# The weight slots of a float32r decoder trunk are moved by 128 bytes in SBUF

## The chip, the cores and the metric

The kernel runs on one core of a Trainium2 chip. The metric is the device time of one execution in microseconds (us), the median of several runs; lower is better. TensorE (PE) multiplies, VectorE (DVE) and ScalarE (ACT) do the elementwise work, GpSimd (POOL) a few small operations, and SyncE (SP) issues the DMAs. Operands of PE lie in SBUF, which has 128 partitions; an address below is a byte offset inside a partition, the same in all partitions.

## The reference

Two layers; in each a SwiGLU half, a mixer and a second SwiGLU half act on a residual stream of 512 tokens by 1024 channels, in float32.

```python
D_MODEL = 1024; SEQ = 512; DEPTH = 2; D_FF = 2816; IN_PROJ_WIDTH = 2560

def _swiglu(h, w_gate, w_up, w_down):
    return (jax.nn.silu(h @ w_gate) * (h @ w_up)) @ w_down

def _mixer(h, w_in, conv_w, pool_w, pool_scale, w_out):
    proj = h @ w_in
    q, k, v, gate_b, gate_c, conv_h, pool_in = jnp.split(proj, SPLIT_POINTS, axis=-1)
    ...
    return jnp.concatenate([attn, conv, pool], axis=-1) @ w_out

def reference(x, norm_g, ffn_w_gate, ffn_w_up, ffn_w_down, w_in, conv_w, pool_w, pool_scale, w_out):
    for l in range(DEPTH):
        g = norm_g[l]
        f = _swiglu(_rmsnorm(x, g[0]), ffn_w_gate[l, 0], ffn_w_up[l, 0], ffn_w_down[l, 0])
        x = x + 0.5 * _rmsnorm(f, g[1])
        m = _mixer(_rmsnorm(x, g[2]), w_in[l], conv_w[l], pool_w[l], pool_scale[l], w_out[l])
        x = x + _rmsnorm(m, g[3])
        f = _swiglu(_rmsnorm(x, g[4]), ffn_w_gate[l, 1], ffn_w_up[l, 1], ffn_w_down[l, 1])
        x = x + 0.5 * _rmsnorm(f, g[5])
    return x
```

The attention is a causal stick-breaking attention of 8 heads of 64 channels; the short convolution has 3 taps, and the pooling mixer applies a 64 by 64 map to each of four groups.

## The kernel before

Every product is made of three float32r matmuls: each operand is split into a high part (rounded to float32r) and a low part (the rest), and high times high, high times low and low times high are summed in PSUM. All of them go through the helper `mm` (L224 in the profile); the order of the matmuls is fixed by hand, since each is made to follow the one before.

The weights are cut into 324 units of 128 partitions by up to 1024 columns. A unit is loaded by a DMA (`load`, L147) into a slot `raw`, ACT rounds it into a second slot `wh` (L155), and DVE subtracts to make `wl` in a third (L156). There are 28 slots of 4096 bytes per partition, in the pool `wpool`. The same slots also hold the hidden layer (`hid`, high part in the first 2048 bytes and low part in the rest), the mixer's `q`, `qk`, `v` and `mix`, the sums `f` and the gains `g`.

The normalised, transposed input of a stage lies in `hh` and `hl` (high and low part, 8 blocks of 512 tokens each, 16384 bytes each), in the pool `cpool`, which stands ahead of the slots. Behind the slots comes `apool` with the temporaries `t`, `pH`, `pL` and `c`.

In a gate, up or input projection (`unit`) the stationary operand of a matmul is a 128 by 128 piece of `wh` or `wl`, and the moving operand a block of `hh` or `hl`, 512 columns (256 in the first blocks of a stage). In a down or output projection (`token_mms`) the stationary operand is a piece of `hid` or `mix` and the moving one 512 columns of `wh` or `wl`. In the `v` projection `hh` or `hl` is stationary and `wh` or `wl` moves. In the attention `pH` and `pL` move over the constants `ntri` and `none_` of `cpool`, and over `v`. A profile's row names the moving operand first: `psz<-hh,wh` has `hh` moving and `wh` stationary. The weights of a matmul are loaded into PE (PEld) while the matmul before it runs, so the two read SBUF at the same time.

`cpool` holds, in this order and each in bytes per partition: `cst` 256, `x` 16384, `mat` 3584, `hh` 16384, `hl` 16384, `ntri`, `none_`, `identr` and `maskr` 512 each, and `expo` 256, of which one column of 4 bytes is used (the exponent of POOL's reciprocal root, L313). From the start of `hh` to the first slot are therefore 16384 + 16384 + 4 x 512 + 256 = 35072 bytes, which is 137 x 256, and from `hl` 73 x 256. Pieces of the operands lie whole multiples of 512 bytes into their tiles. So all the operands named so far begin at the same place modulo 256; only the tiles `c`, 2112 bytes apart, begin elsewhere.

## Time and profile before

| | |
|---|---|
| three runs | 1925.33, 1927.86, 1929.93 us |
| median | 1927.86 us |
| the profiled execution, its own time | 1927.51 us |
| its span from the first to the last instruction | 1925.7 us |
| PE busy | 1884.1 us (98% of the span), 9072 matmuls |
| weight loads (PEld) | 1588.2 us (82%), 9072 |
| DVE busy | 856.5 us (44%) |
| ACT busy | 714.0 us (37%) |
| DMA | 26.7% of 16 engines' span, 178.76 MB |
| PE's granted clock | 0.992 of full on average |

The profiled execution's own time is 1.8 us above its span. Matmuls are pipelined: one of 512 columns lasts some 390 ns in the records, and the next starts before it ends. What one costs in a row of them is therefore read from the distance of their starts, not from their duration.

### The profile page before, as it was taken

To read this page: it belongs to the slowest core of one execution; us is meant where nothing else is said; L and a number is where in the kernel's file an instruction comes from. 1 tells how busy PE (TensorE), PEld (TensorE's weight loads), DVE (VectorE), ACT (ScalarE), POOL (GpSimd) and SP (SyncE) were. 2 spreads that over 40 slices of the span, in tenths; PEclk is the share of its full clock that TensorE was granted. 3 is DMA by queue.
4 is the path that set the end of the run, shared out by engine and by line. 5 is a ranking of instruction groups with operands and counts; after the bars stand their busy time and mean duration, and the time that the engine had idled before them with its cause. 6 is when DMAs were issued, how large, how long until landed. Compare 5 with 4: busy or idle time off the path is not lost.

```text
span 1925.7 us, 21947 instructions
## 1 busy us (share of the span) xinstructions
PE 1884.1 (98%) x9072; PEld 1588.2 (82%) x9072; DVE 856.5 (44%) x1090; ACT 714.0 (37%) x1089; POOL 38.6 (2%) x68
## 2 busy tenths in 40 slices
PE   7999999999998999999999999999999999999998
PEld 6888888888878888888898888887888888888886
DVE  4422343567766323333463232336577563323333
ACT  3323222347764323222342322234577542222221
POOL 0000000000001000000000000000000000000000
PEclk8999999999999999999999999999999999999999
DMA  5323232131123213233142322322111232222311
GB/s 207 110 77 109 85 136 83 60 118 44 44 99 110 99 66 131 78 110 110 44 154 88 109 77 87 133 87 99 67 50 44 83 142 88 100 86 87 132 66 44
DMA packets 50645, 180.17 MB, mean 94 GB/s; under 512 B 5744, under 2 KB 5872, under 8 KB 50544
## 3 DMA queue, kind: packets, MB, share of 16 engines
q1 hardware_dynamic: 50544, 178.76, 26.7%
q8 instruction: 71, 1.16, 0.2%
q14 instruction: 30, 0.25, 0.0%
HBM read 176.65 MB, written 2.10 MB: 93 GB/s over the span
## 4 chain that ended last, share of the span: by engine, by line
PE 92%; DVE 4%; ACT 2%; DMA 1%; issue 1%; SPq 0%; POOL 0%; DVEq 0%; POOLq 0%; ACTq 0%
PE psz L224 80%; PE psd L224 10%; DMA raw<-in_w_dram 1%; DVE wl L156 1%; PE psd L266 1%; ACT t L297 1%; DVE pL L510 0%; DVE t L542 0%; ACT t L539 0%; ACT pH L509 0%; DVE hl L332 0%; DVE f L358 0%; DVE pH L507 0%; ACT wh L155 0%; DVE f L322 0%
## 5 line engine op out<-in xcount | busy, mean ns | idle before, releaser
L224 PE MATMUL psz<-hl,wh 128*128 128x512 f32 (+1 forms) x1536 | 566.9, 369 | 6.3 <-DVE hl L332 5.4
L224 PE MATMUL psz<-hh,wh 128*128 128x512 f32 (+1 forms) x1536 | 567.2, 369 | 4.1 <-ACT hh L331 4.1
L224 PE MATMUL psz<-hh,wl 128*128 128x512 f32 (+1 forms) x1536 | 566.2, 369 | 0.0
L156 DVE TENSOR_TENSOR wl<-raw,wh 128x1024 fp32r<-128x1024 f32 x324 | 386.6, 1210 | 318.1 <-ACT wh L155 248.5
L224 PE MATMUL psz<-wh,hid 128*128 128x512 f32 x1408 | 437.2, 390 | 0.0
L155 ACT CAST wh<-raw 128x1024 fp32r<-128x1024 f32 x324 | 328.7, 1039 | 233.0 <-PE psz L224 178.3
L224 PEld LDWEIGHTS psz<-hl,wh 128*128 128x128 f32 x1536 | 292.4, 190 | 54.6 <-DVE hl L332 6.1
L224 PEld LDWEIGHTS psz<-hh,wh 128*128 128x128 f32 x1536 | 292.2, 190 | 52.2 <-ACT hh L331 5.2
L224 PEld LDWEIGHTS psz<-hh,wl 128*128 128x128 f32 x1536 | 292.2, 190 | 47.5
L224 PEld LDWEIGHTS psz<-wh,hid 128*128 128x128 f32 x1408 | 264.4, 188 | 54.6
L224 PE MATMUL psz<-wl,hid 128*128 128x512 f32 x704 | 274.0, 389 | 0.0
L445 DVE TENSOR_TENSOR t<-t,psz 128x512 f32<-128x512 f32 x84 | 57.7, 687 | 470.5 <-PE psz L224 470.5
L446 ACT CAST hid<-t 128x512 fp32r<-128x512 f32 x88 | 54.6, 620 | 451.0 <-DVE t L445 451.0
L297 ACT ACTIVATE t<-psz 128x512 f32<-128x512 f32 (+1 forms) x136 | 77.5, 572 | 227.2 <-PE psz L224 226.3
L224 PEld LDWEIGHTS psz<-wl,hid 128*128 128x128 f32 x704 | 132.2, 188 | 27.3
L224 PE MATMUL psd<-hh,wh 128*128 128x512 f32 (+1 forms) x320 | 119.7, 374 | 0.0
L224 PE MATMUL psd<-hh,wl 128*128 128x512 f32 (+1 forms) x320 | 118.1, 369 | 0.0
L224 PE MATMUL psd<-hl,wh 128*128 128x512 f32 (+1 forms) x320 | 118.0, 369 | 0.0
L447 DVE TENSOR_TENSOR hid<-t,hid 128x512 fp32r<-128x512 f32 x88 | 60.9, 692 | 60.8 <-ACT hid L446 60.8
L224 PEld LDWEIGHTS psd<-hh,wl 128*128 128x128 f32 x320 | 60.3, 189 | 10.2
L224 PEld LDWEIGHTS psd<-hl,wh 128*128 128x128 f32 x320 | 60.4, 189 | 10.1 <-issue 0.5
L224 PEld LDWEIGHTS psd<-hh,wh 128*128 128x128 f32 x320 | 60.4, 189 | 10.0 <-PE psd L224 0.5
(99 smaller groups left out, 1374.2 us busy)
## 6 DMA issues: line engine op xcount, KB each, us to landing
raw<-in_w_dram SPq DMA_DIRECT2D x316, 512.0 KB, 3.3
g<-in_gains_dram SPq DMA_DIRECT2D x12, 512.0 KB, 5.1
x<-in_xt_dram SPq DMA_DIRECT2D x4, 512.0 KB, 8.4
raw<-in_w_dram SPq DMA_DIRECT2D x8, 256.0 KB, 2.8
out_dram<-x SPq DMA_DIRECT2D x8, 256.0 KB, 2.1
mat<-in_mats_dram SPq DMA_DIRECT2D x1, 384.0 KB, 9.3
mat<-in_mats_dram SPq DMA_DIRECT2D x1, 64.0 KB, 3.2
cst<-in_consts_dram SPq DMA_DIRECT2D x1, 25.0 KB, 9.1
```

Source lines behind the costliest of these rows:

```text
L155: nc.scalar.copy(h[:, :n], raw[:, :n])
L156: nc.vector.tensor_tensor(lo[:, :n], raw[:, :n], f32(h[:, :n]), op=ALU.subtract)
L224: ins = nc.tensor.matmul(dst, w, r, start=start, stop=stop, skip_group_check=True)
L266: ins = nc.tensor.transpose(dst, src, ident)
L297: ins = nc.scalar.activation(out_, in_, f_, **kw)
L445: nc.vector.tensor_tensor(u, g, pu, op=ALU.mult)
L446: nc.scalar.copy(t[:, 0, :], u)
L447: nc.vector.tensor_tensor(t[:, 1, :], u, f32(t[:, 0, :]), op=ALU.subtract)
```

## The change

The tile `expo` is declared 96 columns wide in place of 64. One column of it is used, as before, so 128 bytes more lie unused behind it. The pools behind `cpool` begin 128 bytes later: from `hh` to the first slot are now 35200 bytes, which is 137 x 256 + 128. In the built programs the first slot stands at 71808 before and at 71936 now (128 and 0 modulo 256), while `hh`, `hl` and the constants stay where they were (128 modulo 256). Slots keep their distance from each other and from `t`, `pH`, `pL` and `c`. On every engine the instructions are the same and stand in the same order.

```diff
@@ -194,7 +194,7 @@
     none_ = cpool.tile([P, P], F32R, name="none_")
     identr = cpool.tile([P, P], F32R, name="identr")
     maskr = cpool.tile([P, P], F32R, name="maskr")
-    expo = cpool.tile([P, 64], F32, name="expo")[:, 0:1]
+    expo = cpool.tile([P, 96], F32, name="expo")[:, 0:1]
     nc.vector.memset(expo, -0.5)
```

## Rows read from the trace of the kernel before

**Rows 1.** The page: busy time by engine, granted clock in 40 slices, chain that ended last.

```profile
PE 1884.1 (98%) x9072; PEld 1588.2 (82%) x9072; DVE 856.5 (44%) x1090; ACT 714.0 (37%) x1089; POOL 38.6 (2%) x68
...
PEclk8999999999999999999999999999999999999999
...
PE 92%; DVE 4%; ACT 2%; DMA 1%; issue 1%; SPq 0%; POOL 0%; DVEq 0%; POOLq 0%; ACTq 0%
```

**Rows 2.** The chain in order of time: start us, us, what.

```profile
3.05 8.78 DMA raw<-in_w_dram
...
594.55 5.42 DMA raw<-in_w_dram
...
625.34 14.40 PE psz L224 x120
...
642.62 316.23 PE psz L224 x1395
...
1333.94 5.99 DMA raw<-in_w_dram
...
1543.09 5.24 DMA raw<-in_w_dram
```

**Rows 3.** Timeline of PE, three stretches: start us, us, engine, line, operation, tiles.

```profile
58.80 0.40 PE L224 MATMUL psz<-hh,wh 128*128 128x512 f32 x1
...
113.23 0.39 PE L224 MATMUL psz<-wh,hid 128*128 128x512 f32 x1
...
156.75 0.39 PE L224 MATMUL psz<-hh,wh 128*128 128x512 f32 x1
```

**Rows 4.** Groups of PE, 4.4 to 7.9 us: count | busy us, mean ns | idle before.

```profile
L224 PE MATMUL psd<-t 128*128 128x512 bf16 x17 | 3.8, 379 | 0.0
```

**Rows 5.** Timeline of PE, 4.4 to 7.8 us, the same matmuls.

```profile
4.07 3.83 PE L224 MATMUL psd<-t 128*128 128x512 bf16 x17
```

**Rows 6.** The page: costliest groups of matmuls and weight loads.

```profile
L224 PE MATMUL psz<-hl,wh 128*128 128x512 f32 (+1 forms) x1536 | 566.9, 369 | 6.3 <-DVE hl L332 5.4
...
L224 PEld LDWEIGHTS psz<-hl,wh 128*128 128x128 f32 x1536 | 292.4, 190 | 54.6 <-DVE hl L332 6.1
...
L224 PE MATMUL psd<-hl,wh 128*128 128x512 f32 (+1 forms) x320 | 118.0, 369 | 0.0
```

**Rows 7.** Groups by form of PE and PEld, the smaller ones.

```profile
L224 PE MATMUL psz<-wh,hh 128*128 128x512 f32 x64 | 25.3, 395 | 0.0
...
L224 PEld LDWEIGHTS psz<-pH,none__73 128*128 128x128 f32 x96 | 18.5, 192 | 0.6
...
L224 PEld LDWEIGHTS psz<-pH,ntri 128*128 128x128 f32 x48 | 9.1, 190 | 1.8 <-DVE pH L507 1.2
```

**Rows 8.** Timeline of PE around three of the four products of `c` and `mat`.

```profile
489.69 1.02 PE L224 MATMUL psd<-c,mat 128*128 128x512 f32 x2
...
490.79 0.40 PE L224 MATMUL psd<-hl,wh 128*128 128x512 f32 x1
...
530.59 1.02 PE L224 MATMUL psd<-c,mat 128*128 128x512 f32 x2
...
531.67 0.40 PE L224 MATMUL psz<-pL,v 128*128 128x512 f32 x1
...
1480.98 1.02 PE L224 MATMUL psd<-c,mat 128*128 128x512 f32 x2
...
1482.08 0.40 PE L224 MATMUL psz<-pL,v 128*128 128x512 f32 x1
```

**Rows 9.** DVE's instructions on `c`: count, duration min/median/max, first and last start, forms.

```profile
L694 DVE SCALAR_TENSOR_TENSOR c<-c,c x8: 683/687/690, 476.3 to 1457.5; 64x512 f32<-64x512 f32 x8
...
L661 DVE TENSOR_TENSOR c<-c,psd x4: 676/681/687, 435.7 to 1481.3; 128x512 f32<-128x512 f32 x4
```

**Rows 10.** The page: DMA issues: count, KB each, us to landing.

```profile
raw<-in_w_dram SPq DMA_DIRECT2D x316, 512.0 KB, 3.3
...
raw<-in_w_dram SPq DMA_DIRECT2D x8, 256.0 KB, 2.8
```

## Prediction

> **What bounds the kernel now.** I read the page first. PE is busy for 98% of the span, at nearly full granted clock after the first slice, and 92% of the chain that ended last runs over PE, against 4% over DVE, 2% over ACT and 1% over DMA [rows 1]. The kernel is bound by the rate at which PE gets through its 9072 matmuls. Then I read the chain in order of time, because it shows long unbroken stretches of PE from which that rate follows [rows 2]: 1395 matmuls, gate, up and down mixed, in 316.23 us are 226.7 ns each, and 120 matmuls of 256 columns in 14.40 us are 120.0 ns each. So 256 columns more cost 106.7 ns; 512 columns cost 213.4 ns, and about 13.3 ns is left that every matmul pays whatever its length.

> Is that remainder natural? The 17 warm-up matmuls in bf16 also have 512 columns. They last 3.83 us together [rows 5], the last one its 0.379 us [rows 4], so 16 distances take 3.451 us, 215.7 ns each. A float32r matmul thus pays 11.0 ns more than a bf16 one, and these 11.0 ns are the only thing in the bulk of the kernel that a new place of the operands could touch: they could come from PE reading the next weights and the moving operand from SBUF at once.

> To see whether distance matters already, I split one stretch by kind [rows 3]. From 58.80 to 113.23 us stand 240 gate and up matmuls (5 blocks x 2 weights x 8 pieces x 3 products), `h` moving, weights from a slot: 54.43 us, 226.8 ns each. From 113.23 to 156.75 stand 192 down matmuls (8 blocks x 4 token tiles x 2 halves x 3), both operands in slots: 43.52 us, 226.7 ns each. In the first group the operands lie an odd multiple of 256 bytes apart, in the second an even one. 256 bytes more or less change nothing to 0.1 ns, and neither do the larger distances, which run through all values inside a stretch. But every one of these pairs is 0 modulo 256, so the trace holds no float32r pair at 128.

> **The change part by part.** *Instructions.* None is added, removed or moved, so no wait changes place by order.

> *PE's reads, the disputed term.* The change sets 128 bytes modulo 256 between the two operands of every gate, up and input projection: 3 x 1536 matmuls into `psz` and 3 x 320 into `psd`, 5568 [rows 6]. The `v` projection adds 3 x 64 = 192, and the attention's products with `none_` and `ntri` 2 x 96 + 2 x 48 = 288 [rows 7]; together 6048. The price has no row at 128, so I bound it from both sides. If the 11.0 ns are a conflict of the two reads and the new distance ends it, the gain is 6048 x 11.0 ns = 66.5 us. If instead the new distance brings as much again, the loss is 66.5 us. The nearest rows are those of rows 3, where the distance changes by 256 bytes and the price is 0.1 ns; I take 0. Two more things speak for it. The 13.3 ns are the same in a matmul of 256 and of 512 columns and in every stretch; a meeting of two streams should depend on where they meet. And the four products of `c` and `mat` stand, in the built program, 0, 128, 0 and 64 bytes modulo 256 apart; three are shown [rows 8], at 0, 128 and 64: all last 1.02 us. From their start to the second matmul behind it are 1.10, 1.08 and 1.10 us. They are plain f32, more than 0.4 us for 512 columns, and ask less of SBUF per ns, so this is a hint and no proof; the 0.02 us, if anything, favour 128.

> [...]

> *DVE and ACT.* Instructions on `x` together with `f` or `g`, one side in `cpool` and one in a slot, are now 128 bytes apart modulo 256. The tiles `c` lie 2112 = 8 x 256 + 64 bytes apart, so DVE already works at several distances: eight operations on two such tiles last 683 to 690 ns, four on `c` and PSUM 676 to 687 [rows 9], a spread of 1.6% at most. DVE and ACT hold 6% of the chain, 116 us, so even 1% on all of it is 1.2 us. I take 0, with 1.2 us either way; it hides under PE elsewhere, where DVE is busy 44% of the span.

> *DMA.* The slots now begin at 0 modulo 256 in absolute terms. 512 KB land in 3.3 us and 256 KB in 2.8 [rows 10], so the 256 KB more cost 0.5 us and the moving of 512 KB about 1.0. The chain waits four times for a `raw` [rows 2]; a tenth of 1.0 us on each is 0.4 us in all. I take 0, with 0.4 us either way.

> [...]

> *Sum.* 1927.5 us of the profiled execution (span 1925.7 and 1.8 around it), plus 0, with 1.6 us from the small terms either way. That execution lies 0.4 us under the median, in the spread of the three runs (1925.3 to 1929.9). Prediction 1927.5 us, by itself 1924 to 1931.

> **The rivals.** *Faster: the 11.0 ns are a conflict, and 128 ends it.* For it: float32r pays them and bf16 doesn't, and the 0.02 us beside `c`. Against it: 226.7 and 226.8 ns at two kinds of distance, and a remainder that is the same in every stretch. All of it gives 1927.5 - 66.5 = 1861 us; the down projections would stay at 226.7 ns.

> *Slower: 0 modulo 256 is the good place, and at 128 the weight load and the moving stream meet.* Place: each matmul of the gate, up and input projections, where the next weights are read beside the stream. For it: all these pairs now lie at 0, so the trace doesn't say what another place costs, and the weight loads, 190 ns in the records [rows 6], run beside nearly every stream; PE has no slack to take it in. Against it: the same rows as for the faster one, and the pair of `c` and `mat` at 128. It decides as soon as one such matmul loses 0.7 ns (3.9 us over 6048). Half as much again as now, 5.5 ns, gives 1961 us; the full doubling 1994 us.

> *The change doesn't do what it says.* A pool that rounds tiles up to 256 bytes would move the slots by 256. The built program has them 128 further, so I leave this out.

> **How the numbers follow.** About 0.2%, 3.9 us, is what a measurement of this kernel can tell from no change. No change: 0.62, from the equal rows at two distances and the clean remainder. Slower: 0.22, the larger of the two rest chances because a loss has no bound in the trace while a gain ends at 11.0 ns. Faster: 0.16. The predicted time is that of the likeliest case. The range leaves out the faster case alone, 0.16: it begins at 1922, a little under the likeliest case's own lower end, and goes to the full doubling, 1994.

> **What would show it.** In the changed kernel the first 240 gate and up matmuls should again take 54.4 us and the 192 down matmuls behind them 43.5. If the first number falls toward 51.8 (215.7 ns each) with the second unchanged, the 11.0 ns were a conflict and the faster rival holds; if it grows to 55.7 or 57.1 with the second unchanged, the slower one does. If both move alike, the absolute place of the slots counts, not their distance from `h`. DVE's split of a unit (L156) and ACT's rounding (L155) should stay within 1%. The prediction is wrong if the distance of starts in the gate and up stretches changes by more than 0.7 ns.

## The result and the profile after

The kernel became slower by 1.3%: 1952.27 us, median of four runs (1951.91 to 1954.85), against 1927.33 us for four runs of the kernel before; ratio 1.013, 95% interval 1.0118 to 1.0142. The profiled execution took 1951.91 us with a span of 1950.1 us, 24.4 us more than before.

The page of the changed kernel (busy time, granted clock, chain), to be held against [rows 1]:

```profile
PE 1911.8 (98%) x9072; PEld 1587.0 (81%) x9072; DVE 857.2 (44%) x1090; ACT 713.3 (37%) x1089; POOL 39.8 (2%) x68
...
PEclk8999999999999999999999999999999999999999
...
PE 92%; DVE 4%; ACT 2%; DMA 1%; issue 1%; POOL 0%; SPq 0%; DVEq 0%; POOLq 0%; ACTq 0%
```

PE is busy 27.7 us longer with the same 9072 matmuls at nearly the same granted clock (0.994 of full on average for 0.992), DVE and ACT within 1 us of before. The chain in order of time (start us, us, what), against [rows 2]:

```profile
58.11 322.32 PE psz L224 x1395
...
601.07 4.71 DMA raw<-in_w_dram
...
631.03 14.24 PE psz L224 x120
...
648.12 322.08 PE psz L224 x1395
...
1019.79 322.08 PE psz L224 x1395
...
1609.77 332.29 PE psz L224 x1440
```

The first, third and fourth of these stretches in the chain of the kernel before:

```profile
58.97 316.23 PE psz L224 x1395
...
1008.64 316.23 PE psz L224 x1395
...
1591.22 326.44 PE psz L224 x1440
```

The stretch of 1395 matmuls took 316.23 us and takes 322.08 to 322.32. The fourth stretch, of 1440, took 326.44 us and takes 332.29. Four times 5.85 to 6.09 us are 23.6 us, nearly all of the 24.4 us that the span grew by. The 120 matmuls of 256 columns became a little shorter, 14.24 us for 14.40.

PE's timeline at the ends of the first gate and up matmuls and of the down matmuls behind them, as in [rows 3]:

```profile
57.95 0.39 PE L224 MATMUL psz<-hh,wh 128*128 128x512 f32 x1
...
113.95 0.39 PE L224 MATMUL psz<-wh,hid 128*128 128x512 f32 x1
...
157.49 0.40 PE L224 MATMUL psz<-hh,wh 128*128 128x512 f32 x1
```

The 240 gate and up matmuls take 56.00 us, 233.3 ns each (226.8 before). The 192 down matmuls, whose operands both lie in slots and kept their distance, take 43.54 us, 226.8 ns each, as before. The loss is where the slower rival put it, and the down matmuls beside it show none. Inside such a stretch the matmuls no longer follow each other evenly (timeline of PE):

```profile
99.95 0.39 PE L224 MATMUL psz<-hh,wh 128*128 128x512 f32 x1
100.18 0.40 PE L224 MATMUL psz<-hl,wh 128*128 128x512 f32 x1
100.42 0.39 PE L224 MATMUL psz<-hh,wl 128*128 128x512 f32 x1
100.65 0.40 PE L224 MATMUL psz<-hh,wh 128*128 128x512 f32 x1
100.88 0.39 PE L224 MATMUL psz<-hl,wh 128*128 128x512 f32 x1
101.11 0.40 PE L224 MATMUL psz<-hh,wl 128*128 128x512 f32 x1
```

In the records the distances of starts alternate between 229 and 237 or 238 ns in most of the stretch; before, all but 5 of 239 were 225 to 228. The mean is 233.3 ns. PE waits for no other engine in such a stretch (0.0 us from 58.2 to 380 us), and what DVE and ACT do beside it makes no difference above 0.5 ns: over the whole trace, where both were idle beside a matmul the mean was 233.2 ns over some 1950 matmuls, and where both were busy for at least 95% of it 232.7 over 565.

### The profile page after: what moved, and what is told of

Read it like the earlier page. It is cut to its first block, busy times and chain, and to the rows that moved or that the text cites. A ratio compares the mean times of both kernels' runs of the same rounds, so it can differ in the third digit from the quotient of the medians.

```text
span 1950.1 us, 21947 instructions
## 1 busy us (share of the span) xinstructions
PE 1911.8 (98%) x9072; PEld 1587.0 (81%) x9072; DVE 857.2 (44%) x1090; ACT 713.3 (37%) x1089; POOL 39.8 (2%) x68
## 4 chain that ended last, share of the span: by engine, by line
PE 92%; DVE 4%; ACT 2%; DMA 1%; issue 1%; POOL 0%; SPq 0%; DVEq 0%; POOLq 0%; ACTq 0%
PE psz L224 80%; PE psd L224 11%; DMA raw<-in_w_dram 1%; DVE wl L156 1%; PE psd L266 1%; ACT t L297 1%; DVE pL L510 0%; DVE t L542 0%; DVE hl L332 0%; ACT t L539 0%; ACT pH L509 0%; DVE f L322 0%; ACT wh L155 0%; POOL ss L313 0%; DVE pH L507 0%
## 5 line engine op out<-in xcount | busy, mean ns | idle before, releaser
L224 PE MATMUL psz<-hl,wh 128*128 128x512 f32 (+1 forms) x1536 | 573.6, 373 | 6.4 <-DVE hl L332 5.5
L224 PE MATMUL psz<-hh,wh 128*128 128x512 f32 (+1 forms) x1536 | 574.0, 374 | 2.9 <-ACT hh L331 2.9
L224 PE MATMUL psz<-hh,wl 128*128 128x512 f32 (+1 forms) x1536 | 573.0, 373 | 0.0
L156 DVE TENSOR_TENSOR wl<-raw,wh 128x1024 fp32r<-128x1024 f32 x324 | 386.8, 1210 | 321.8 <-ACT wh L155 248.9
L155 ACT CAST wh<-raw 128x1024 fp32r<-128x1024 f32 x324 | 328.4, 1037 | 233.6 <-PE psz L224 178.9
```

Source lines behind the costliest of these rows:

```text
L155: nc.scalar.copy(h[:, :n], raw[:, :n])
L156: nc.vector.tensor_tensor(lo[:, :n], raw[:, :n], f32(h[:, :n]), op=ALU.subtract)
L224: ins = nc.tensor.matmul(dst, w, r, start=start, stop=stop, skip_group_check=True)
```

## Experiments

The theory after the result: PE pays for the distance, modulo 256, between the moving operand and the weights that are read beside it. The rivals: the absolute place of the slots (now 0 modulo 256) or of `h`; another engine's traffic to the slots; a matmul's own weights rather than those loaded beside it. Distances below are those of the slots from `h`: the address of the slots less that of `h`, modulo 256. The price of a run is read from its first chain stretch of 1395 matmuls, in which 912 are gate and up (240, 384 and 288): (stretch - 316.23 us) / 912.

**The place or the distance.** In e1 everything moves by 128 bytes, in e2 only `h` and the constants, in e3 the slots by 256, in e4 by 64.

```diff
# e1
-    cst = cpool.tile([P, 64], F32, name="cst")[:, :C_END]
+    cst = cpool.tile([P, 96], F32, name="cst")[:, :C_END]
# e2: the same line, and
-    expo = cpool.tile([P, 64], F32, name="expo")[:, 0:1]
+    expo = cpool.tile([P, 32], F32, name="expo")[:, 0:1]
# e3, e4: expo alone, 128 and 80 columns wide
```

> cst is declared 96 columns wide and expo stays at 64: h, the constants and the slots all begin 128 bytes later, at 0 modulo 256, and their distance is that of the kernel before. If the distance between the moving h and the weights sets the price, the gate and up matmuls are back at 226.7 ns (240 in about 54.4 us) and the time at 1927 us. If the absolute place of the slots (0 modulo 256) sets it, they stay at 233.3 ns and the time at 1952 us. If the place of h sets it, neither number is excluded.

> cst 96 and expo 32 columns wide: the slots stand exactly where they stood in the kernel before, and h and the constants 128 bytes later, so the distance is 128 modulo 256 with the other sign. Distance theory: 233 ns in the gate and up matmuls, 226.7 in the down ones, 1952 us as after the change. Theory that the place of the slots counts: 226.7 ns and 1927 us.

> expo 128 columns wide: the slots begin 256 bytes later than in the kernel before. If the distance counts modulo 256, this is the kernel before, 226.7 ns and 1927 us; if only the number of bytes added counts, or the distance modulo 512, the gate and up matmuls differ from both 226.7 and 233.3 ns.

> expo 80 columns wide: distance 64 modulo 256. If the price rises with the distance up to 128, the gate and up matmuls come between 226.7 and 233.3 ns, near 230, and the time near 1940 us. If 128 is a bad place of its own and all others are like 0, 226.7 ns and 1927 us. If 0 is the only good place, 233 ns and 1952 us.

Measured, single runs beside 1924.81 us for the kernel before: e1 1928.95, e2 1957.50, e3 1927.28, e4 1956.47 us. The first long stretch in the chain of each (start us, us, what):

Chain of e1, `h` and slots both at 0:

```profile
57.79 316.23 PE psz L224 x1395
```

Chain of e2, `h` moved, slots in their old place:

```profile
59.15 322.09 PE psz L224 x1395
```

Chain of e3, distance 256:

```profile
58.66 316.23 PE psz L224 x1395
```

Chain of e4, distance 64:

```profile
57.88 322.36 PE psz L224 x1395
```

With the slots at 0 modulo 256 and `h` there too (e1) the stretch is that of the kernel before to the last digit; with the slots back in their old place and `h` moved (e2) it is that of the changed kernel. So the distance counts, and neither place. 256 bytes more are the same as none (e3). At 64 the price is as high as at 128 (e4): (322.36 - 316.23) / 912 = 6.7 ns. The times of e2 and e4 lie 4 to 5 us above the changed kernel's, but not in these stretches: e2 has 3.6 us more than the changed kernel between the first long stretch and the 120 matmuls of the next FFN. In that part of the run (372 to 640 us) the mean granted clock of TensorE is 0.97 in e2, and in e4 too, and 0.99 in the changed kernel (over the whole run 0.989, 0.989 and 0.994): both spend some 10 us more at half of the full clock. By estimate that costs up to half of 10 us: at a granted clock of 0.50 the changed kernel's matmuls of 256 columns start 213 ns apart, for 119 at the full clock. So the clock is the likely source of the difference; no run separates it.

**Other distances.** The line of `expo` again: 72 columns (e5, distance 32), 88 (e7, 96), 104 (e11, 160), 112 (e6, 192) and 120 (e10, 224).

> expo 72 columns wide: distance 32 modulo 256. Distances 64 and 128 cost the same, 233.3 ns in the gate and up matmuls. If every distance but 0 costs that, 233 ns and 1952 to 1957 us. If the good place has some width around 0, 226.7 ns and 1927 us.

> expo 112 columns wide: distance 192 modulo 256, which is 64 on the other side. If only the size of the distance counts, as 64: 233 ns and 1956 us. If the order of the two streams counts (weights ahead of or behind the moving operand), another number, perhaps 226.7 ns and 1927 us.

> expo 88 columns wide: distance 96 modulo 256, between two distances that cost 233 ns. Every distance but 0 is bad: 233 ns, 1952 to 1957 us. Places that alternate (multiples of 64 alike, odd multiples of 32 apart): another number, as distance 32 has.

> expo 120 columns wide: distance 224 modulo 256, 32 on the other side. The v projection of the run at distance 32, where stream and weights have changed places, took 233.3 ns: if the signed distance alone decides, the gate and up matmuls take 233 ns here, 1955 us. If 192 is good because it is on the side where the weights lie ahead of the stream, 229 ns or less, below 1936 us.

> expo 104 columns wide: distance 160 modulo 256. The v projection at distance 96, with the places changed, took 233.3 ns: by the signed distance 233 ns and 1955 us; by the side alone 229 ns and 1936 us.

The same stretch in the chain of each:

Chain of e5, distance 32:

```profile
58.26 322.35 PE psz L224 x1395
```

Chain of e7, distance 96:

```profile
57.92 323.22 PE psz L224 x1395
```

Chain of e11, distance 160:

```profile
56.97 322.44 PE psz L224 x1395
```

Chain of e6, distance 192:

```profile
58.17 318.43 PE psz L224 x1395
```

Chain of e10, distance 224:

```profile
58.39 322.40 PE psz L224 x1395
```

| distance | 0 | 32 | 64 | 96 | 128 | 160 | 192 | 224 |
|---|---|---|---|---|---|---|---|---|
| price of a gate or up matmul, ns | 0 | 6.7 | 6.7 | 7.7 | 6.7 | 6.8 | 2.4 | 6.8 |
| time, us | 1927.3 | 1956.1 | 1956.5 | 1960.1 | 1952.3 | 1954.0 | 1935.7 | 1957.3 |

The times at 0 and 128 are the medians above, the others single runs with a scatter of some us. Neither the size of the distance nor its side decides: 224 is as bad as 32, and 192 is mild though 64 is not. What decides is the signed distance, weights less stream modulo 256: in the `v` projection, where stream and weights change places, the run at 64 has 229.1 ns, the run at 192 has 233.3 and those at 32 and 96 have 233.3 (means of some 186 matmuls, settling included), as the gate and up matmuls have at the opposite distances.

**One part of `h` alone.** `hl` (e8) or `hh` (e12) begins 128 bytes inside a tile that is 256 bytes longer, so that the other part and the constants stay at distance 0.

```diff
# e8; e12 does the same to hHs and "hh" instead
-    hLs = cpool.tile([P, KB, T], F32R, name="hl")
+    hLs = cpool.tile([P, KB * T + 64], F32R, name="hl")[:, 32:32 + KB * T]
+    hLs = hLs.rearrange("p (a b) -> p a b", b=T)
```

> Only the low part hl is moved by 128 bytes inside a tile that is 256 bytes larger; hh and the constants keep distance 0 to the slots. One matmul in three of the gate and up stretches then streams at distance 128. If each matmul pays for its own distance to the weights that are loaded beside it, a third of 6.6 ns is added on the mean, 228.9 ns, and 1935 us. If one bad distance spoils the rhythm of its neighbours, the mean comes near 233 ns and the time near 1952 us.

> Only the high part hh is moved by 128 bytes inside its tile, hl keeps distance 0 to the slots: two matmuls in three of the gate and up stretches stream at distance 128. If each pays for itself, 226.7 plus two thirds of 6.6, 231 ns, and 1944 us, hl at 227 and hh at 233 ns. If neighbours are spoiled, 233 ns for all and 1952 us.

Measured: e8 1938.17 us (before 1926.83), e12 1938.61 us (before 1928.62). Over the whole trace of e8 the matmuls that stream `hl` take 233.3 ns and those that stream `hh` 228.4; in e12 it is 226.1 for `hl` and 230.4 for `hh`. The same stretch again (these kernels are a line longer, so `mm` is L225):

Chain of e12, `hh` moved:

```profile
58.85 318.36 PE psz L225 x1395
```

Chain of e8, `hl` moved:

```profile
57.67 318.78 PE psz L225 x1395
```

The price follows the operand that was moved, but it doesn't add up by the matmul. In e8 a third of the matmuls is out of place and 2.8 ns are lost on the mean of this stretch, not 2.2; in e12 two thirds are, and only 2.3 ns are lost, not 4.4. The expectation for e12 was missed. Nor is the price of one distance fixed: the third such stretch of e8 takes 319.30 us with the same matmuls at the same distances, 0.5 us more than the first, and the changed kernel has 322.08 and 322.32. So what a matmul pays depends on those before it as well; the rule of that sequence was not found.

**PE alone.** A program with one stream, one tile of weights behind it (2048 bytes each), and nothing of the reference but the copy of `x`; 48 matmuls to a group. The weights begin `o` bytes into their tile, 16 bytes more from group to group, so `o` is the distance modulo 256. The helper that makes a group, cut from its kernel:

```python
def group(name, n, cols, offsets, count=48, l=w, r=s, size=4):
    ps = ppool.tile([P, 512], F32, tag="z", bufs=8, name=name)
    for i in range(count):
        o = offsets[i % len(offsets)] // size
        mm(ps[:, :cols], l[:, o:o + P], r[:, :cols])
```

> No part of the reference is computed: PE alone runs groups of 48 float32r matmuls of 512 columns with one stream and weights whose distance to it grows by 16 bytes from group to group (dista 0, distb 16, ... distp 240), then groups of 96 with 256 columns (halfa, halfe, halfi, halfm at 0, 64, 128, 192), a group whose weights alternate between 0 and 128 (turn), and bf16 at 0 and 128 (bfa, bfi). If the price is a meeting of PE's own two reads, it is here without DVE, ACT and DMA: 226.7 ns at 0, 233 ns at 32, 64, 96 and 128, 229 at 192, and bf16 the same 215.7 ns at both. If DVE, ACT or the DMAs are part of it, every group takes 226.7 ns. In the group turn, what is read beside a stream is the next matmul's weights: if they count, the matmul with the weights at 0 is the long one; if its own weights count, the one with those at 128.

The timeline of PE in e9 (start us, us, tiles, count). A group of 48 holds 47 distances and one matmul's own 0.39 us, so 11.04 us are 226.6 ns each and 11.36 us are 233.4.

```profile
10.34 11.04 PE L122 MATMUL dista<-stream,weights 128*128 128x512 f32 x48
21.21 11.05 PE L122 MATMUL distb<-stream,weights 128*128 128x512 f32 x48
32.10 11.35 PE L122 MATMUL distc<-stream,weights 128*128 128x512 f32 x48
...
65.69 11.29 PE L122 MATMUL distf<-stream,weights 128*128 128x512 f32 x48
76.81 11.40 PE L122 MATMUL distg<-stream,weights 128*128 128x512 f32 x48
...
99.24 11.36 PE L122 MATMUL disti<-stream,weights 128*128 128x512 f32 x48
...
143.88 11.15 PE L122 MATMUL distm<-stream,weights 128*128 128x512 f32 x48
...
177.26 11.06 PE L122 MATMUL distp<-stream,weights 128*128 128x512 f32 x48
188.16 11.67 PE L122 MATMUL halfa<-stream,weights 128*128 128x256 f32 x96
199.67 11.47 PE L122 MATMUL halfe<-stream,weights 128*128 128x256 f32 x96
...
244.86 10.53 PE L122 MATMUL bfa<-bstream,bweights 128*128 128x512 bf16 x47
255.23 10.52 PE L122 MATMUL bfi<-bstream,bweights 128*128 128x512 bf16 x47
```

The kernel's numbers come back with no other engine at work (the copy of `x` ends during `dista`): 226.6 ns at 0 (`dista`), 234.3 at 96 (`distg`), 233.4 at 128 (`disti`), 228.9 at 192 (`distm`). Good places are 0, 16 (`distb`) and, after three matmuls of settling, 240 (`distp`); 80 (`distf`) with 231.9 ns, 176 (not shown) with 229.9 and 192 lie between. The ten other places have 233.2 to 234.3. In bf16 the two groups, at 0 and 128, differ by 0.01 us (one record of 48 is missing in each), so bf16 shows no price at 128. With 256 columns, where one matmul's own time is 0.28 us, it is the other way round: 119.9 ns at 0 (`halfa`), 117.8 at 64 (`halfe`), and, not shown, 118.7 at 128 and 117.8 at 192. The group that alternates between 0 and 128 gave uneven intervals and doesn't tell whose weights count; hence the next run.

> No part of the reference is computed: PE alone again, 512 columns unless said. Distances 0, 4, 8, 12 and 20 bytes (nought, four, eight, twelve, twenty): if the two reads meet by whole lines of 16 bytes or more, 226.7 ns up to 12; if some place frees PE of the whole remainder, one of them comes near 215.7. oneineight: seven matmuls with weights at 0, then one with weights at 128. If the weights that are loaded beside a stream count, the interval before the odd matmul grows first; if a matmul's own weights count, the odd matmul's own interval does. oneback: the same with 128 as the rule and 0 as the exception. twostreams: every eighth stream moved by 128 bytes, weights fixed: its own interval is the long one by both readings. longa, longi, longm: 384 columns at 0, 128 and 192, where 173.3 ns (160 and 13.3) stand at 0; if the price at 128 is a fixed 6.7 ns, 180. stepb and stepc: weights with every second or third column read, so that their place relative to the stream drifts: 226.7 to 234 ns if only the place counts, more if a line that is left early costs.

The timeline of PE in e13, read in the same way:

```profile
10.89 11.05 PE L123 MATMUL nought<-stream,weights 128*128 128x512 f32 x48
21.78 11.32 PE L123 MATMUL four<-stream,weights 128*128 128x512 f32 x48
32.94 11.24 PE L123 MATMUL eight<-stream,weights 128*128 128x512 f32 x48
44.02 11.20 PE L123 MATMUL twelve<-stream,weights 128*128 128x512 f32 x48
...
110.41 11.28 PE L123 MATMUL longa<-stream,weights 128*128 128x384 f32 x64
121.53 11.43 PE L123 MATMUL longi<-stream,weights 128*128 128x384 f32 x64
...
143.89 11.36 PE L123 MATMUL stepb<-stream,weights 128*128 128x512 f32 x48
```

4, 8 and 12 bytes already cost: 232.4, 230.7 and 229.9 ns, from the starts themselves; 20 bytes, not shown, have 233.3. None of the three places tried between 0 and 16 is good, and with 512 columns no place tried is better than 0. With 384 columns, 128 bytes cost 2.3 to 2.7 ns (173.7 for 0, or 173.3 without its first six intervals, and 176.0 for 128), so the price of 128 bytes grows with the length of the stream: less than nothing at 256 columns, 2.5 at 384, 6.7 at 512. Weights of which only every second column is read cost 6.8 ns too (`stepb`). With every third column (`stepc`, not shown) a matmul takes 235.4 ns, more than at any distance, and its weight load 253 ns for 188 in the other groups; the expectation had put more than 234 ns down to lines that are left early, which no run tests. Whose weights count is read from the two groups with one exception in eight; these are the mean distances, in ns from a matmul's start to the next one's, by place in the eight (the last place is the exception; the first eight are left out). In `twostreams` the weights stay and the stream is the exception:

```
oneineight (weights at 0 0 0 0 0 0 0 128)          226.6 226.7 226.7 226.6 226.7 226.7 232.3 234.3
oneback    (weights at 128 128 ... 128 0)          240.7 232.6 230.7 231.7 228.3 230.0 226.7 232.6
twostreams (stream at 0 0 0 0 0 0 0 128)           226.0 227.0 226.0 227.0 227.0 226.0 227.0 234.0
```

In `oneineight` the interval before the odd matmul grows by 5.6 ns; in it the stream runs over weights at 0 while those at 128 are loaded. In `oneback` the only good interval, 226.7 ns, is the one in which the weights at 0 are loaded beside a stream over weights at 128. Both say that the weights loaded beside the stream count. The odd matmul's own interval in `oneineight`, 234.3 ns, doesn't follow from that, since the weights loaded in it lie at 0. It could be left over from the disturbed matmul before it; but in `twostreams` the disturbed matmul, 234.0 ns, is followed at once by one of 226.0. So this part of the reading stays open.

**No share of the place.** e1's kernel once more, timed.

> The kernel with h, constants and slots all at 0 modulo 256, timed against the kernel before in the same job. If nothing but the distance counts, no difference beyond 0.2%. If the place of the slots or of h by itself has a small share, up to the 4 us that the single look showed, 0.2% slower.

1928.33 us (10 runs) against 1925.79 (13 runs), ratio 1.0007, interval 0.9996 to 1.0017: no difference that can be told. The 4 us of the single run were scatter.

## Why the prediction failed

**What bounds the kernel** was right: PE is the chain before and after, and the whole change came out of the rate at which it runs.

**PE's reads.** This step failed. The prediction took 0 for the price at 128, from the rows at an even and an odd multiple of 256 bytes and from the remainder being the same everywhere. The rows were right and the inference was not. All the pairs of the trace lay at one single place modulo 256, so that their agreement tested nothing but whole multiples of 256, over which the price repeats (e3: 316.23 us for the stretch, as before). The measured price is 6.7 ns, inside the bounds of 11.0 ns either way and on the side of the slower rival. The measured 1952.27 us lie inside the stated range only because that rival, at a chance of 0.22, had stretched it to 1994; the likeliest case, no change at 0.62, was the wrong one.

The loss added up from the records: 4346 distances behind `hh` or `hl` with 512 columns (those under 260 ns) rose from 226.9 to 233.1 ns on the mean, 26.9 us; the `v` projection adds 192 x 5.3 ns, 1.0 us, and 1152 matmuls of 256 columns give back 1.3 ns each, 1.5 us. That is 26.4 us, 2.0 more than the span grew by. PE's idle time became 3.3 us shorter (span less busy time, 41.6 us before and 38.3 after), and its mean granted clock was 0.994 for 0.992; how much each of them gave wasn't separated. With PE alone the price comes back (e9: 226.6 ns at 0, 233.4 at 128), so the two reads of PE are where it arises; in what part of their path they disturb each other no run shows.

**The argument from length** ("the same in a matmul of 256 and of 512 columns") was wrong too: the price of 128 bytes depends on length, with its sign: -1.2 ns at 256 columns (e9), 2.5 at 384 (e13), 6.7 at 512. It had been drawn from the remainder at distance 0 alone.

**`c` and `mat`** were no hint. In the changed kernel their pairs lie at 128, 0, 128 and, counted to the nearer side, 64, and from their start to the second matmul behind it are 1.08 us at 128 and 1.09 at 0 (timeline of PE in the changed kernel, distance 128 first):

```profile
496.62 1.02 PE L224 MATMUL psd<-c,mat 128*128 128x512 f32 x2
...
497.70 0.39 PE L224 MATMUL psd<-hl,wh 128*128 128x512 f32 x1
...
538.10 1.02 PE L224 MATMUL psd<-c,mat 128*128 128x512 f32 x2
...
539.19 0.40 PE L224 MATMUL psz<-pL,v 128*128 128x512 f32 x1
```

So plain f32 shows no price above 0.01 us in these pairs. It isn't excluded at every distance: in e6, with the slots at 192, two of the four pairs start 434 ns apart and the other two 428, which is not explained. The prediction named the reason for doubt, fewer bytes per ns (the two matmuls of a pair start 428 or 429 ns apart in both traces), and still counted the pairs as speaking for 0.

**DVE, ACT and DMA** were right at 0. DVE's split has a median of 1225 ns (1224 before), ACT's rounding one of 1047 (1049 before), the eight operations on two `c` tiles last 684 to 691 ns against 683 to 690 in [rows 9], and 512 KB land in 3.3 us as in [rows 10]. The chain's waits for a `raw` are some tenths of a us shorter where they recur (4.71 for 5.42 us), but the way to them has changed too, so this doesn't show that the transfers gained from their new place.

**The rivals.** The slower one had the place and the sign; its price lies a little above half of the doubling that it allowed, and the down projections stayed at 226.8 ns as its test wanted. The faster one is excluded for 512 columns at every distance tried: no place brings the 11.0 ns back that a float32r matmul takes above a bf16 one. What they are stays open: bf16 takes 215.7 ns in the warm-up and 215.8 in e9, and float32r 226.7 even at its best place.

## What to carry to other kernels

Where float32r matmuls of 512 columns bound a kernel, let the tiles that stream and the tiles of weights begin at the same place modulo 256 bytes (226.8 ns a matmul here, and 233.3 at 128), and pad odd small tiles so that what stands behind them keeps it; the down projections (226.8 ns with the slots moved, 226.7 before) and e1 (its stretch takes 316.23 us, as before) show no price of the place itself. For 256 columns this doesn't hold: there 0 was the dearest of the four distances tried (e9: 119.9 ns, and 117.8 to 118.7 at the others). When a trace is asked whether something matters, see first whether it has ever varied: rows that agree over one single value of a quantity say nothing of the others. Stretches that a change leaves alone, as the down projections here, are the best control, and they stand in the same trace.
